# Modulation rows by column groups, half products ahead of the layer, and a new order on VectorE in a two-layer hybrid block

## The chip, the cores and the metric

One core of one Trainium2 chip. The metric is device time in microseconds; 2223.8 us is the median of three runs of the kernel before (2223.27 to 2225.72). A change of about 0.2% can be told from none.

## The reference, cut to what matters

```python
for i in range(DEPTH):                                   # 2 layers
    mod_l = (jax.nn.silu(c) @ w_mod[i] + b_mod[i])       # 6 x 1024 numbers, from one row
    mod_c = (jax.nn.silu(c_ctx) @ w_mod[i] + b_mod[i])   # the same for the context
    sh1, sc1, g1, sh2, sc2, g2 = jnp.split(mod_l, N_MOD, axis=-1)
    zl = _split_cols(_modulate(x, sh1, sc1) @ w_in[i])   # layernorm * (1 + sc1) + sh1
    zc = _split_cols(_modulate(h_ctx, csh1, csc1) @ w_in[i])
    # four mixers (retention, HGRN2, gated DeltaNet, RG-LRU) over context, then latents
    y_l = _merge([ret_l, hg_l, gd_l, lr_l], zl['merge_gate'], w_branch[i], w_out[i])
    x = _layernorm(alpha * x + g1 * y_l, ln_mix_g[i], ln_mix_b[i])
    f_l = _conv_ffn(_modulate(x, sh2, sc2), w_up[i], ffn_conv[i], ffn_conv_b[i], w_down[i])
    x = _layernorm(alpha * x + g2 * f_l, ln_ffn_g[i], ln_ffn_b[i])
    # the same for h_ctx in all layers but the last
```

There are 256 latent and 256 context tokens, D is 1024, the FFN 2816 wide. The gated DeltaNet's `qkv` columns go through a depthwise convolution over the tokens of a segment.

## The kernel before, in words

**Products.** Each large product streams one tile of weights (128 x 1024 numbers, 512 KB, tile `wraw`) from memory over SP's queue. ScalarE (ACT) copies it rounded into `wH` and VectorE (DVE) or GpSimd (POOL) subtracts to get the rest, `wL` (`splitter`, line 386). The activations `xm` are held as `xmH` and `xmL` (`xms` in layer 1). A product is then three passes: wH by xH, wH by xL, wL by xH. `gemm_ft` (line 687) puts weights in the array and streams tokens, `gemm_tf` and `gemm_tw` the other way round; results lie in three PSUM banks (`pgt`, line 520) until an **eviction** (`evac`, line 471) has read them: a convolution for `gft` and `up`, a residual add (`gy`, then `r`, then statistics `st`; `add_y`, line 945) for the `gtf` of w_out and w_down.

**The order is planned.** `pump` (line 297) writes one program order for each engine. Every piece of work is a generator (thread) that yields the engine and tiles it next needs; `account` keeps a clock for each engine, `when` (line 337) says when a thread could go on, and `pump` takes the one with the smallest start, less a lead and less the thread's fourth entry, its priority, if it is ready by the time the engine is free. Before, only the layernorm threads (`LN_FIRST`, 1.0) have a priority. Jobs of products run in the order of a list; a job at the head of it that is not `ready` holds back all behind it. `_Job.strict` stops a later one from overtaking.

**Modulation.** `mod_jobs` (line 781): silu(c) is a column pair `cz`, padded to 32; w_mod comes in 24 blocks (`nb` 0 to 11 of each layer) of 512 columns, each in four jobs. A job streams 256 columns for four parts of the contraction at once, each part into its own 32 partitions of the PSUM tile `modp`. After the fourth job ACT copies `modp` (128 x 512) to `modrow`, and the four parts are summed by products with a selection matrix `sel`: four products into `modcp` where the result is needed as columns (shift and scale, then DVE's `modc`), one into `modr` where it is needed as a row (the gates, then `modbm` to memory). Blocks 0, 2, 1, 3 of layer 0 are the head (`early`); 13 blocks are fillers, one job after each weight tile; blocks 6 and 7 of layer 1 come behind the first `up` jobs of layer 0, 4 and 5 at the start of layer 1, 9 to 11 in its middle (`LATE`).

**Head and layernorms.** `modulate` (line 851) does statistics, normalises, transposes (`xmt`) and modulates two segments, sg 0 the context and sg 1 the latents, eight blocks of 128 channels each. In layer 0 the first products are six of the gated DeltaNet, each as a pair (`both`, line 1793): first the context's 256 tokens, then the latents' with the weight tile loaded and split a second time. At the end of a sublayer `mid` and `end` (lines 1235 and 1249) do post-layernorm and `modulate` of segment 0 while the last product of segment 1 is on TensorE (PE).

All instructions go through one wrapper, so the profile puts them on line 85: rows are told apart by tile names.

Of the kernel before, what the change touches and what calls it, by code (L numbers as in the profile page):

```python
# [35 lines left out]
NWR = 4  # L36
# [12 lines left out]
LN_FIRST = 1.0  # L49
SPLIT_FIRST = 0.0  # L50
# [10 lines left out]
NBR = (1, 2)  # L61
NIN = (6, 5)
# [55 lines left out]
class Net:  # L118
    def __init__(self, nc, tc, I, out, n_tiles, dbg=None, stop=None):
        self.nc, self.tc, self.I, self.out = nc, tc, I, out  # L120
        self.specs = []
        self.n_tiles = n_tiles
        self.dbg = dbg or {}
        self.stop = stop
        self.PE, self.A, self.V = _Eng(self, nc.tensor, "PE"), _Eng(self, nc.scalar, "ACT"), _Eng(self, nc.vector, "DVE")
        self.G, self.S = _Eng(self, nc.gpsimd, "POOL"), _Eng(self, nc.sync, "SP")
        self.clk = dict(PE=0.0, ACT=0.0, DVE=0.0, POOL=0.0, SP=0.0, DMA=0.0)
        self.rdy, self.rd, self.base, self.slots, self.hw, self.by_seg, self.sto = {}, {}, {}, {}, 0.0, set(), {}
        self.table, self.n_ran = "exp", 0
# [4 lines left out]
        self.raws, self.plain, self.open, self.ok, self.masks_ok = 0, False, {}, set(), False  # L134
        self.want, self.dma_q, self.ready_q, self.n_wt = [], [], [], 0

# [200 lines left out]
    def when(self, t):  # L337

        w = t[1]
        if callable(w):  # L340
            return "PE", (0.0 if w() else None)
        key, w = w[:2] if isinstance(w, tuple) else ("PE", w)
        if key == "tt":
            key = "DVE" if self.clk["DVE"] < self.clk["POOL"] + 1.0 else "POOL"
        return key, max([max(self.after(self.rdy, y, key), self.base.get(y, 0.0)) for x in (w or []) for y in self.names(x)] + [0.0])
# [22 lines left out]
    def feed(self):  # L368

        while len(self.want) + len(self.dma_q) + len(self.ready_q) < (10 if self.jobs and self.jobs[0].early else 4):  # L370
            if not self.pick():
                break
        while self.want and self.raws < (8 if self.want[0][1].early else NWR):
# [9 lines left out]
            self.dma_q.append((raw, w, job.mode))  # L383
            self.raws += 1

    def splitter(self):

        while True:
            yield lambda: len(self.ready_q) < NWH - 1 and len(self.dma_q) > 0
            raw, w, mode = self.dma_q.pop(0)  # L390
            if mode == "plain":
                self.ready_q.append((raw, None))
# [8 lines left out]
            self.ready_q.append((H, L))  # L401
# [27 lines left out]
    def next_tile(self):  # L429
        if self.plain:  # L430
# [5 lines left out]
        self.plain = r[1] is None  # L436
        self.feed()
        return r
# [32 lines left out]
    def evac(self, rec, ps, f, eng="ACT"):  # L471

        job = self.cur
        job.pend += 1

        def run():
            yield eng, [ps]
            r = f(ps)
            if r is not None:
                yield from r  # L480
            job.pend -= 1
        t = self.spawn(run())
        rec.append(t)
        t[2] = True
# [74 lines left out]
    def load_consts(self):  # L559
# [4 lines left out]
        self.sel_c = const.tile([128, 2], F32, name="sel")  # L564
        S.dma_start(self.sel_c, I["c_sel"])
# [121 lines left out]
    def gemm_ft(self, ps, HL, xH, xL, K, w=128, c0=0):  # L687
# [4 lines left out]
        for k in range(K):  # L692
            h = H[:, k * w + c0:k * w + c0 + 128]
            for p, x in enumerate(xH(k) + xL(k)):

                mm(ps[:, x[1]:x[1] + x[0].shape[-1]], h, x[0], start=(k == 0 and p == 0), stop=False)
            n += 2
            if n % 4 == 0:
                yield
        for k in range(K):  # L700
            xs = xH(k)
            for p, x in enumerate(xs):
                mm(ps[:, x[1]:x[1] + x[0].shape[-1]], L[:, k * w + c0:k * w + c0 + 128], x[0], start=False,
                   stop=(k == K - 1 and p == len(xs) - 1))
# [4 lines left out]
    def in_ft(self, i, c0, tsl, evac, cond=None):  # L709
# [9 lines left out]
        jb.ready = self.seen(i, 0, tsl.start, tsl.stop)  # L719
        return jb  # L720
# [60 lines left out]
    def mod_jobs(self, i, nb, early=False):  # L781
# [4 lines left out]
        def mk(kk):  # L786
            def run():
                if kk == 0:
                    if early:
                        st["row"] = self.tile(self.fw, [128, 512], F32, "f_row", "modrow", 4)  # L790
                        st["ps"], st["rec"] = self.pgt([128, 512], "modp")
                    else:
                        if self.mod_th is not None:
                            self.finish(self.mod_th)
                        st["row"] = None
                        st["ps"], st["rec"] = self.tile(self.pq, [128, 512], F32, "modp", "modp", 1), []
                W, ps = self.next_tile()[0], st["ps"]
                half, kh = kk % 2, kk // 2
# [9 lines left out]
            def evac(ps):  # L808
                row = st["row"] if early else self.ev([128, 512], "modrow")
                self.A.activation(row, ps, AF.Copy)  # L810
                kind = nb // 2
                if kind in (2, 5):
                    half, c0 = kind // 3, (nb % 2) * 512
                    yield "PE", [row], "free"
                    pr = self.pmt([128, 512], "modr")
                    mm(pr[0:2, :], self.sel_c, row, start=True, stop=True)
# [4 lines left out]
                    self.V.tensor_tensor(bm, bm, pr[0:2, :], op=ALU.add)  # L821
# [3 lines left out]
                yield "PE", [row], "free"  # L825
                kind = {0: 0, 1: 1, 3: 2, 4: 3}[kind]
                pc = self.pmt([128, 4, 2], "modcp")
# [4 lines left out]
                self.V.scalar_tensor_tensor(self.modc[i][:, kind, j0:j0 + 4, :], in0=pc, scalar=float(kind % 2),  # L832
                                            in1=self.par[i][:, b0:b0 + 4].unsqueeze(2).broadcast_to([128, 4, 2]), op0=ALU.add, op1=ALU.add)
            j = _Job([(("w_mod", i, nb * 512 + (kk % 2) * 256, 4, 256, (kk // 2) * 4), 1024)], run)
# [16 lines left out]
    def modulate(self, i, half, sg, xs):  # L851
# [25 lines left out]
        for d in range(0, 8, 2):  # L877
# [19 lines left out]
            self.tt(L, x32, H.bitcast(F32), op=ALU.subtract)  # L897
            yield xn
# [46 lines left out]
    def add_y(self, cs, sg, js, ps, al, stats):  # L945
# [9 lines left out]
        V.tensor_tensor(tmp, ps, self.grow[sg][:, cs].unsqueeze(1).broadcast_to([128, n, 512 // n]), op=ALU.mult)  # L955
        V.scalar_tensor_tensor(r, in0=r, scalar=al, in1=tmp, op0=ALU.mult, op1=ALU.add)
# [16 lines left out]
    def body(self):  # L973
# [11 lines left out]
        xs = {}  # L985
        for sg, nm in ((0, "ctx"), (1, "x")):
# [3 lines left out]
        self.A.dma_start(self.ck, self.I["c_f32"])  # L990
# [4 lines left out]
        self.fill = rest  # L995
# [790 lines left out]
    def gdn_jobs(self, inst, g):  # L1786
# [6 lines left out]
        def both(make, t0):  # L1793

            if g == 0 and t0 == 0:
# [6 lines left out]
        for m, dst in ((g, ("yqk", 0)), (2 + g, ("yqk", 1)), (4 + 2 * g, ("yv", 0)), (5 + 2 * g, ("yv", 1))):  # L1802
            def make(t0, t1, m=m, dst=dst):
# [10 lines left out]
                return self.in_ft(i, COL["gdn_qkv"] + m * 128, slice(t0, t1), ev, cond)  # L1814
# [363 lines left out]
N_TILES = 485 + 2 * SPLIT_UP  # L2178
# [9 lines left out]
def _constants():  # L2188
# [22 lines left out]
    sel = np.zeros((128, 2), np.float32)  # L2211
    for j in range(2):
        sel[j::32, j] = 1.0
    c["c_sel"] = sel
# [33 lines left out]
def _host_arrays(a, specs):  # L2248
# [13 lines left out]
    for i in range(DEPTH):  # L2262
# [19 lines left out]
        for d in range(2):  # L2282
            for ty, nm in enumerate(("lru_w_a", "lru_w_i")):
# [11 lines left out]
               c_msk=(128, 416), c_sel=(128, 2), c_rope=(128, 2, 256),  # L2295
# [25 lines left out]
```

## Time and profile before

| | |
|---|---|
| median of three runs | 2223.8 us |
| the profiled execution, its own time | 2219.78 us |
| its span, first to last instruction | 2218.0 us |
| mean granted TensorE clock | 0.965 of 2.4 GHz |
| busy: PE, DVE, ACT, POOL | 2039.0, 1495.4, 868.6, 427.3 us |

The rows further down are from this one execution. A row of a timeline gives start, length, engine, operation, result <- operands, shape, count, and in brackets the idle time just before with what ended it. Matmul lengths overlap: the cost of one in a stream is the distance of two starts.

### The profile page before, as it was taken

To read this page: it belongs to the slowest core of one execution; us is meant where nothing else is said; L and a number is where in the kernel's file an instruction comes from. 1 tells how busy PE (TensorE), PEld (TensorE's weight loads), DVE (VectorE), ACT (ScalarE), POOL (GpSimd) and SP (SyncE) were. 2 spreads that over 40 slices of the span, in tenths; PEclk is the share of its full clock that TensorE was granted. 3 is DMA by queue.
4 is the path that set the end of the run, shared out by engine and by line. 5 is a ranking of instruction groups with operands and counts; after the bars stand their busy time and mean duration, and the time that the engine had idled before them with its cause. 6 is when DMAs were issued, how large, how long until landed. Compare 5 with 4: busy or idle time off the path is not lost. (4 is left out here: it accounts for less than half of the span.)

```text
span 2218.0 us, 33680 instructions
## 1 busy us (share of the span) xinstructions
PE 2039.0 (92%) x13236; PEld 1749.5 (79%) x13236; DVE 1495.4 (67%) x2520; ACT 868.6 (39%) x1277; POOL 427.3 (19%) x442
## 2 busy tenths in 40 slices
PE   6999999999999999789999976998989999879997
PEld 4766777788889878678898865887978989867895
DVE  6787565445738368986646678787476566778786
ACT  4555331322222323344314434556332333326562
POOL 0163216220101001200000022273225221200000
PEclk9999999999999999889999998999999999989999
DMA  7544434424141567462223244354324422566553
GB/s 298 201 133 150 154 124 129 129 98 140 67 136 64 170 217 241 148 218 95 98 93 98 97 147 166 108 169 119 120 96 130 142 72 63 184 245 229 176 185 109
DMA packets 129679, 319.35 MB, mean 144 GB/s; under 512 B 29136, under 2 KB 51568, under 8 KB 129520
## 3 DMA queue, kind: packets, MB, share of 16 engines
q1 hardware_dynamic: 128000, 312.17, 42.7%
q0 software_dynamic: 832, 2.54, 0.4%
q8 instruction: 104, 1.70, 0.3%
q10 hardware_dynamic: 688, 2.49, 0.3%
q14 instruction: 55, 0.45, 0.1%
HBM read 294.05 MB, written 23.10 MB: 143 GB/s over the span
## 5 line engine op out<-in xcount | busy, mean ns | idle before, releaser
L85 DVE TENSOR_TENSOR wL<-wraw,wH 128x1024 fp32r<-128x1024 f32 (+2 forms) x339 | 419.4, 1242 | 172.9 <-ACT wH L85 167.6
L85 ACT ACTIVATE wH<-wraw 128x1024 fp32r<-128x1024 f32 (+1 forms) x395 | 407.9, 1036 | 233.3 <-PE gtf L85 150.7
L85 POOL TENSOR_TENSOR wL<-wraw,wH 128x1024 fp32r<-128x1024 f32 (+2 forms) x56 | 131.5, 2350 | 933.7 <-ACT wH L85 860.0
L85 PE MATMUL gft<-xmH,wH 128*128 128x512 f32 (+1 forms) x544 | 215.4, 400 | 7.4 <-DVE g_th L85 3.8
L85 PE MATMUL gft<-xmL,wH 128*128 128x512 f32 (+1 forms) x544 | 205.2, 382 | 0.0
L85 PE MATMUL gft<-xms,wH 128*128 128x256 f32 x1344 | 188.5, 292 | 8.0 <-DVE gd_yv L85 2.8
L85 PEld LDWEIGHTS gft<-xms,wH 128*128 128x128 f32 x1344 | 173.5, 197 | 15.4 <-issue 11.2
L85 DVE SCALAR_TENSOR_TENSOR ffy<-up,parf,ffy 128x255 f32<-128x255 f32 (+1 forms) x188 | 110.8, 589 | 74.7 <-ACT ffy L85 70.3
L85 PE MATMUL up<-xmL,wH 128*128 128x512 f32 (+1 forms) x400 | 144.4, 369 | 3.5 <-DVE xmL L85 3.5
L85 PE MATMUL up<-xmH,wH 128*128 128x512 f32 (+1 forms) x400 | 144.0, 368 | 0.0
L85 PEld LDWEIGHTS gft<-xmH,wH 128*128 128x128 f32 x544 | 103.1, 190 | 46.7 <-issue 17.5
L85 PE MATMUL gft<-xmH,wL 128*128 128x512 f32 (+1 forms) x544 | 133.2, 383 | 1.2 <-DVE wL L85 0.9
L85 PE MATMUL gtf<-wH,hidH 128*128 128x256 f32 (+1 forms) x352 | 114.4, 341 | 16.4 <-DVE gy L85 15.7
L85 PE MATMUL gtf<-wH,xmH 128*128 128x256 f32 (+1 forms) x384 | 109.8, 313 | 13.9 <-DVE gy L85 11.9
L85 PEld LDWEIGHTS gft<-xmL,wH 128*128 128x128 f32 x544 | 103.3, 190 | 17.4 <-issue 0.7
L85 PEld LDWEIGHTS gft<-xmH,wL 128*128 128x128 f32 x544 | 97.3, 189 | 20.9 <-DVE wL L85 1.1
L85 PE MATMUL gtf<-wH,hidL 128*128 128x256 f32 (+1 forms) x352 | 113.8, 340 | 0.0
L85 PE MATMUL gtf<-wH,xmL 128*128 128x256 f32 (+1 forms) x384 | 106.1, 303 | 0.0
L85 PE MATMUL gft<-xms,wL 128*128 128x256 f32 x672 | 99.1, 293 | 5.0 <-POOL wL L85 4.9
L85 ACT ACTIVATE ffy<-up,parf 128x256 f32<-128x256 f32 (+1 forms) x94 | 61.3, 652 | 107.4 <-PE up L85 106.8
L85 PE MATMUL up<-xms,wH 128*128 128x256 f32 x704 | 93.0, 285 | 2.0 <-ACT wH L85 1.8
L85 PE MATMUL mg_b<-brH,wH 128*128 128x256 f32 (+1 forms) x288 | 89.8, 332 | 5.2 <-ACT brH L85 3.1
(327 smaller groups left out, 4291.7 us busy)
## 6 DMA issues: line engine op xcount, KB each, us to landing
wraw<-in_wt SPq DMA_DIRECT2D x475, 512.0 KB
thd<-mg_t SPq DMA_DIRECT2D x32, 256.0 KB
mg_th<-thd SPq DMA_DIRECT2D x32, 256.0 KB
lnw<-in_rows SPq DMA_DIRECT2D x8, 512.0 KB
thd<-mg_t SPq DMA_DIRECT2D x32, 128.0 KB
xmm<-thd SPq DMA_DIRECT2D x16, 256.0 KB
brd<-ro_b SPq DMA_DIRECT2D x28, 128.0 KB
ret_tab<-in_c_ret SPq DMA_DIRECT2D x16, 192.0 KB
```

The lines of the kernel that those rows point to most:

```text
L85: r = f(*a, **k)
```

## The change

- A modulation job now holds two parts of the contraction and all 512 columns; each 128 columns go to their own 32 partitions of a 128 x 128 `modp`. Eight matmuls of 128 columns take the place of four of 256. Nothing is left to sum: `modrow` is 128 x 128, `modcp` is one PE transposition, `modr` four matmuls of 128 columns with two columns of the identity each. `sel` and its load are gone. The head's blocks share the one `modp` tile with the others, and a block's first job first finishes the block before.
- Three of the gated DeltaNet's tiles in layer 0 (`HEAD`) are computed in two halves: `head_ft` over the first four channel blocks as soon as these are modulated for both segments, `rest_ft` over the others. Two halves stand before block 3 of the modulation, one after it. In layer 0 the pairs are gone: all 512 tokens are one job, and seven weight tiles are not loaded a second time (481 tiles with the three more of the halves, 485 before).
- Evictions get priority 2.0 (`EVAC_FIRST`). `add_y` yields between its product and its sum, `modulate` between the statistics of its blocks.
- The transposition of a block that is not early may follow 3 us later (`LATER`).
- The constants `ck` are loaded on ACT's queue ahead of the two inputs instead of behind them. Early tiles have a count of buffers of their own (`raws0`).

```diff
+EVAC_FIRST = 2.0
+LATER = 3.0
+HEAD = tuple(COL["gdn_qkv"] + m * 128 for m in (0, 2, 4))
...
+        lag = w[3] if isinstance(w, tuple) and len(w) > 3 else 0.0
...
-        return key, max([...] + [0.0])
+        return key, max([...] + [0.0]) + lag
...
-        while len(self.want) + len(self.dma_q) + len(self.ready_q) < (10 if self.jobs and self.jobs[0].early else 4):
+        while len(self.want) + len(self.dma_q) + len(self.ready_q) < (10 if self.head else 4):
...
-        t = self.spawn(run())
+        t = self.spawn(run(), EVAC_FIRST)
...
-    def gemm_ft(self, ps, HL, xH, xL, K, w=128, c0=0):
+    def gemm_ft(self, ps, HL, xH, xL, K, w=128, c0=0, first=True, last=True):
...
+    def head_ft(self, c0):
+        def run():
+            HL = self.next_tile()
+            self.parts[c0] = self.pgt([128, 512], "gft")
+            yield from self.gemm_ft(self.parts[c0][0], HL, *self.xf(0, 512), 4, last=False)
+        jb = _Job([(("w_in", 0, c0, 4, 128, 0), 512)], run)
+        jb.ready = lambda: all((0, 0, sg, "half") in self.ok for sg in range(2))
+        return jb
+    def rest_ft(self, c0, evac, cond):
+        def run():
+            HL = self.next_tile()
+            ps, rec = self.parts.pop(c0)
+            xs = [lambda k, x=x: x(k + 4) for x in self.xf(0, 512)]
+            yield from self.gemm_ft(ps, HL, *xs, 4, first=False)
+            self.evac(rec, ps, evac)
...
-                for k in range(4):
-                    mm(ps[32 * k:32 * k + 32, half * 256:half * 256 + 256], self.cz[:, kh * 4 + k, :], W[:, k * 256:(k + 1) * 256],
-                       start=(kk == 0), stop=(kk == 3))
+                for k in range(2):
+                    for j in range(4):
+                        mm(ps[32 * j:32 * j + 32, :], self.cz[:, kk * 2 + k, :], W[:, k * 512 + j * 128:k * 512 + (j + 1) * 128],
+                           start=(kk == 0 and k == 0), stop=(kk == 3 and k == 1))
...
-                    mm(pr[0:2, :], self.sel_c, row, start=True, stop=True)
+                    for j in range(4):
+                        mm(pr[0:2, j, :], self.ident[:, 32 * j:32 * j + 2], row, start=True, stop=True)
...
-                yield "PE", [row], "free"
+                yield "PE", [row], "free", 0.0 if early else LATER
...
-                for j in range(4):
-                    mm(pc[:, j, :], row[:, j * 128:(j + 1) * 128], self.sel_c, start=True, stop=True)
+                self.PE.transpose(pc.rearrange("p j c -> p (j c)"), row, self.ident)
...
                 V.bn_stats(st[:, j, q, :], xs[j][:, q * 512:(q + 1) * 512])
+            yield "DVE", [st]
...
+            if d == 2:
+                self.ok.add((i, half, sg, "half"))
...
         V.tensor_tensor(tmp, ps, self.grow[sg][:, cs].unsqueeze(1).broadcast_to([128, n, 512 // n]), op=ALU.mult)
+        yield "DVE", [tmp], "free"
...
+        hd = [self.head_ft(c0) for c0 in HEAD]
+        early[12:12] = hd[:2]
+        early.append(hd[2])
...
-            if g == 0 and t0 == 0:
+            if g == 0 and t0 == 0 and i > 0:
...
+                return self.rest_ft(c, ev, cond) if i == 0 and c in HEAD else self.in_ft(i, c, slice(t0, t1), ev, cond)
```

## Rows read from the trace of the kernel before

**Rows 1.** The page's part 1: engine, busy us, share, instructions.

```profile
PE 2039.0 (92%) x13236; PEld 1749.5 (79%) x13236; DVE 1495.4 (67%) x2520; ACT 868.6 (39%) x1277; POOL 427.3 (19%) x442
```

**Rows 2.** The waits of PE: total us, times, longest.

```profile
PE gtf L85 <- DVE gy L85: 27.7, 6, 11.9
...
PE modr L85 <- ACT modrow L85: 12.8, 2, 12.0
...
PE modcp L85 <- ACT modrow L85: 7.3, 7, 1.8
...
PE gft L85 <- DVE g_th L85: 6.3, 3, 2.5
```

**Rows 3.** PE's timeline in the head, 21 to 48 us.

```profile
21.74 1.08 PE L85 MATMUL modp<-wraw,cz 128*32 128x256 f32 x8 [0.20 <-DMA wraw<-in_wt]
22.75 1.87 PE L85 MATMUL modcp<-sel,modrow 128*128 128x2 f32 x8
...
35.35 1.94 PE L85 MATMUL modp<-wraw,cz 128*32 128x256 f32 x32
38.00 1.05 PE L85 MATMUL modcp<-sel,modrow 128*128 128x2 f32 x8 [0.72 <-ACT modrow L85]
38.92 1.94 PE L85 MATMUL xmt<-ck,x 128*128 128x128 f32 x16
...
44.34 0.39 PE L85 MATMUL gft<-xmH,wH 128*128 128x256 f32 x1 [2.91 <-ACT wH L85]
...
47.97 0.64 PE L85 MATMUL modp<-wraw,cz 128*32 128x256 f32 x8
```

**Rows 4.** DVE's timeline in the head: last of the first and of the second half.

```profile
35.42 0.69 DVE L85 TENSOR_TENSOR xmL<-xm,xmH 128x512 fp32r<-128x512 f32 x1
...
47.24 0.99 DVE L85 TENSOR_SCALAR xm<-xmt,modc 128x256 f32<-128x256 f32 x2
```

**Rows 5.** PE's groups by form: matmuls into 64 partitions at a time; busy, mean ns.

```profile
L85 PE MATMUL gd_pw<-gd_T,gd_ek 128*64 128x128 f32 x128 | 8.8, 279 | 0.1
```

**Rows 6.** The timeline around the layernorm behind w_out of layer 0.

```profile
902.89 2.43 POOL L85 TENSOR_TENSOR wL<-wraw,wH 128x1024 fp32r<-128x1024 f32 x1 [0.26 <-ACT wH L85]
...
903.10 2.24 DVE L85 TENSOR_TENSOR rq<-rq_i 128x2 f32<-128x2 f32 x1
...
920.85 0.80 PE L85 MATMUL gtf<-wH,xmH 128*128 128x512 f32 x1 [11.94 <-DVE gy L85]
...
933.35 0.69 DVE L85 TENSOR_TENSOR xmL<-xm,xmH 128x512 fp32r<-128x512 f32 x1
...
935.15 0.28 PE L85 MATMUL up<-xmH,wH 128*128 128x256 f32 x1
...
939.42 0.99 DVE L85 SCALAR_TENSOR_TENSOR ffy<-up,parf,ffy 128x255 f32<-128x255 f32 x2
```

**Rows 7.** The timeline from the last products of layer 0 into layer 1.

```profile
1298.26 1.23 DVE L85 TENSOR_TENSOR wL<-wraw,wH 128x1024 fp32r<-128x1024 f32 x1 [0.41 <-ACT wH L85]
...
1300.23 0.47 PE L85 MATMUL gtf<-wH,hidH 128*128 128x512 f32 x1 [1.47 <-DVE gy L85]
...
1325.74 0.77 PE L85 MATMUL gtf<-wH,hidH 128*128 128x512 f32 x1 [9.87 <-DVE gy L85]
...
1338.22 0.69 DVE L85 TENSOR_TENSOR xms<-xm,xms 128x512 fp32r<-128x512 f32 x1
...
1343.47 2.08 PE L85 MATMUL gft<-xms,wH 128*128 128x256 f32 x16
...
1370.85 1.01 PE L85 MATMUL modr<-modrow,sel 128*2 128x512 f32 x1 [12.03 <-ACT modrow L85]
...
1381.45 1.22 PE L85 MATMUL gft<-xms,wH 128*128 128x256 f32 x4 [2.21 <-ACT wH L85]
```

**Rows 8.** Busy us by stretch: length, PE, PEld, DVE, ACT, POOL; granted clock, DMA, GB/s.

```profile
1301.00:1384.40 83.40, 56.10 (x326) 42.00 (x325) 72.43 (x134) 29.93 (x47) 25.71 (x12) 0.86 0.44 144
901.00:975.00 74.00, 54.46 (x343) 45.19 (x342) 68.40 (x123) 28.82 (x43) 15.94 (x7) 0.81 0.48 164
```

More of the change, by code (lines that the diff above doesn't have):

```diff
@@ L344, in when @@
             key = "DVE" if self.clk["DVE"] < self.clk["POOL"] + 1.0 else "POOL"
-        return key, max([max(self.after(self.rdy, y, key), self.base.get(y, 0.0)) for x in (w or []) for y in self.names(x)] + [0.0])
+        return key, max([max(self.after(self.rdy, y, key), self.base.get(y, 0.0)) for x in (w or []) for y in self.names(x)] + [0.0]) + lag
     def take(self, j):
@@ L382, in feed @@
             self.n_wt += 1
-            self.dma_q.append((raw, w, job.mode))
-            self.raws += 1
+            self.dma_q.append((raw, w, job.mode, job.early))
+            if job.early:
+                self.raws0 += 1
+            else:
+                self.raws += 1
     def splitter(self):
@@ L435, in next_tile @@
         r = self.ready_q.pop(0)
-        self.plain = r[1] is None
+        self.plain = r[1] is None and ("early" if r[2] else "late")
         self.feed()
-        return r
+        return r[:2]
     def drain(self, jobs):
@@ L694, in gemm_ft @@
             for p, x in enumerate(xH(k) + xL(k)):
-                mm(ps[:, x[1]:x[1] + x[0].shape[-1]], h, x[0], start=(k == 0 and p == 0), stop=False)
+                mm(ps[:, x[1]:x[1] + x[0].shape[-1]], h, x[0], start=(first and k == 0 and p == 0), stop=False)
             n += 2
@@ L703, in gemm_ft @@
                 mm(ps[:, x[1]:x[1] + x[0].shape[-1]], L[:, k * w + c0:k * w + c0 + 128], x[0], start=False,
-                   stop=(k == K - 1 and p == len(xs) - 1))
+                   stop=(last and k == K - 1 and p == len(xs) - 1))
             n += 1
@@ L719, in in_ft @@
         jb.ready = self.seen(i, 0, tsl.start, tsl.stop)
+        return jb
[6 more added lines that the diff above has]
+        jb.ready = lambda: all((0, 0, sg, "half") in self.ok for sg in range(2))
+        return jb
+    def rest_ft(self, c0, evac, cond):
[5 more added lines that the diff above has]
+            self.evac(rec, ps, evac)
+        jb = _Job([(("w_in", 0, c0, 4, 128, 4), 512)], run, cond)
+        jb.strict = True
+        jb.ready = self.seen(0, 0, 0, 512)
         return jb
@@ L788, in run @@
                 if kk == 0:
[L789 to L796, printed above, removed]
+                    if self.mod_th is not None:
+                        self.finish(self.mod_th)
+                    st["ps"], st["rec"] = self.tile(self.pq, [128, 128], F32, "modp", "modp", 1), []
                 W, ps = self.next_tile()[0], st["ps"]
-                half, kh = kk % 2, kk // 2
-                for k in range(4):
-                    mm(ps[32 * k:32 * k + 32, half * 256:half * 256 + 256], self.cz[:, kh * 4 + k, :], W[:, k * 256:(k + 1) * 256],
-                       start=(kk == 0), stop=(kk == 3))
+                for k in range(2):
+                    for j in range(4):
+                        mm(ps[32 * j:32 * j + 32, :], self.cz[:, kk * 2 + k, :], W[:, k * 512 + j * 128:k * 512 + (j + 1) * 128],
+                           start=(kk == 0 and k == 0), stop=(kk == 3 and k == 1))
                 if kk == 3:
@@ L808, in evac @@
             def evac(ps):
-                row = st["row"] if early else self.ev([128, 512], "modrow")
+                row = self.tile(self.fw, [128, 128], F32, "f_row", "modrow", 4) if early else self.ev([128, 128], "modrow")
                 self.A.activation(row, ps, AF.Copy)
@@ L813, in evac @@
                     half, c0 = kind // 3, (nb % 2) * 512
-                    yield "PE", [row], "free"
-                    pr = self.pmt([128, 512], "modr")
-                    mm(pr[0:2, :], self.sel_c, row, start=True, stop=True)
+                    yield "PE", [row], "free", LATER
+                    pr = self.pmt([128, 4, 128], "modr")
+                    for j in range(4):
+                        mm(pr[0:2, j, :], self.ident[:, 32 * j:32 * j + 2], row, start=True, stop=True)
                     bm = self.ev([2, 512], "modbm")
@@ L819, in evac @@
                     yield "DVE", [bm, pr]
-                    self.V.tensor_tensor(bm, bm, pr[0:2, :], op=ALU.add)
+                    self.V.tensor_tensor(bm, bm, pr[0:2].rearrange("p j c -> p (j c)"), op=ALU.add)
                     self.V.tensor_scalar(bm, bm, 0.5, None, op0=ALU.mult)
@@ L994, in body @@
         self.close(self.fw)
-        self.fill = rest
+        self.fill, self.head = rest, False
         self.S.dma_start(self.msk.bitcast(F32), self.I["c_msk"])
```

36 lines of the change are left out of this document (16 added, 20 removed).

## The prediction

> **What bounds the kernel now.** First the page's busy shares: PE is busy 92% of the span [rows 1], so some 180 us of it can be won without making products cheaper. Then the waits of PE, to see behind whom they lie: the residual add `gy` (27.7 us, of which one wait is 11.9), the modulation row `modrow` (12.8 and 7.3 us), `g_th` (6.3 us) [rows 2]. These are the waits at which the change aims. Then the timeline around the long ones, and there the reader is to see what comes next. The 11.94 us behind `gy` end at 920.85, but the first `up`, for which w_out is only in the way, starts at 935.15, and its last operand `xmL` is written at 933.35 plus 0.69 [rows 6]. The layernorm's chain on DVE ends with PE's work, stall included. The same in layer 0's end: a wait of 9.87 us ends at 1325.74, the last `xms` of segment 0 comes at 1338.22, the first product of layer 1 at 1343.47; then 12.03 us behind `modrow`, and the latents' products only at 1381.45 [rows 7]. Last the busy times of the two stretches: DVE is busy 68.4 of 74.0 us and 72.4 of 83.4 [rows 8]. **In both DVE's work, not its order, is nearly the bound**; 5.6 and 11.0 us are idle.
>
> **The sum** is made against the profiled execution's 2219.78 us (span 2218.0 and 1.8 around it); the median is 4.0 above it. What the sum changes I take off the median.
>
> *Modulation, sums gone.* A `modcp` of four products takes PE from 38.00 to 38.92, so 0.92 us; a transposition costs a sixteenth of 1.94, 0.12 [rows 3]. 0.8 us are saved each of 16 times. Four are in the head (below), three (blocks 6, 7, 9 of layer 1) where PE waits anyway: 9 x 0.8 = **-7.2**. `modr` streams 512 columns before and after: 0, at most eight more short records, under 1 us. `modrow` and its PSUM read shrink to a quarter; ACT is 39% busy, so 0 outside the head.
>
> *Modulation, more matmuls.* A job has 16 records instead of 8, each half as long. Four jobs of 8 records take 1.94 us, one alone 0.64, so a job in a stream costs (1.94 - 0.64) / 3 = 0.43 [rows 3]. The columns streamed are the same, so no gain. For a loss, the nearest row with 128 columns goes two groups at a time: 8.8 us / 128 = 69 ns each [rows 5]; by the 0.43 us it would be 53, so 16 ns are extra, times 16 records 0.25 us a job, times 52 filler jobs 13 us. I take 0.05 us a job, since the row with four groups shows nothing extra: **+2.6**, with 0 and +13 as ends. The other 44 jobs lie in the head, where a tile lands every 1.28 us (1.08 busy and 0.20 of waiting) and a job takes 1.08 [rows 3], or where PE waits for DVE.
>
> The Trainium skill (TensorE: Matmul & The Clock Gate, LDWEIGHTS) says that a load of weights takes its columns divided by 1.2 in ns, 27 ns for 32, which speaks against the change: it makes twice as many. If none were hidden, my estimate from that page is 8 x 27 ns x 52 = 11.2 us in the place of 2.6, and the sum would be -12.3. The trace's 0.43 us a job says that they are hidden when four groups run in turn.
>
> *The head.* Before, PE does its first real product at 44.34 [rows 3], though the first half of the channels is modulated for both segments at 35.42 + 0.69 = 36.1; the second half ends about 48.9 (47.24, 0.99 and the 0.69 of an `xmL`) [rows 4]. In the chain to the first half, `modcp` costs 1.87 us [rows 3], twice: some 2.5 us fall away, and ACT reads a quarter. So halves start at about 34. One is 12 matmuls of 512 columns; 16 of 256 take 2.08 [rows 7], 1.92 without the tail, so 12 of twice the width some 2.8 us. But two of them now stand on PE ahead of block 3, whose jobs ran at 35.35: its `modcp` ends at about 42 instead of 39 (38.00 and 1.05), and the second half at about 50 instead of 48.9. The context's pairs, which ran from 44.34, have to wait for that too. At 50 PE has done 8.4 us of halves where before it had done 5.8 (two context products), and from there all weights lie ready and both segments with them, where before PE stalled several times. The pairs gone spare some 1.5 us of PE, seven splits and half the fixed cost of three convolution steps on DVE. I take **-4** (ends -9 and +4: block 3 later still). Moved queues: `ck` ahead of `ctx` and `x` on ACT's queue puts 384 KB before them, 0.75 of the 1.28 us in which a tile lands [rows 3]: statistics begin 1 us later, hidden by the modulation's tiles, the eighth of which is used at 21.74 [rows 3]; without that cover 1 us. On SP's queue two half tiles stand ahead of block 3's last tiles, also some 1.3 us, and are in the 42 above.
>
> *Transpositions later.* The 7.3 us that `modcp` waits for `modrow` are seven waits of at most 1.8 [rows 2]; some lie in the head and next to layernorms. Where PE is the bound: **-1.8**, ends 0 and -3. The 12.03 us stay outside: the next block needs the one `modp` tile, so the row must be read first, and PE has no real product before 1381.45.
>
> *Evictions first, behind w_out.* `gy` would go at about 909 instead of 920, so the 11.94 us [rows 6] go. Late next is the layernorm: its chain now has three more evictions ahead of it (each three steps of 512 columns, 0.69 us a step as the `xmL` of that width, 2.1 in all) and, since PE does not stop, POOL's splits beside it. A `rq` of two numbers took 2.24 us beside such a split [rows 6]. So PE waits for `xmL` instead, and `up` starts at 935 to 943; but segment 1's evictions are done earlier, which gives time back by 975. **-1**, ends -5 (DVE's idle time) and +8.
>
> *The same at the end of layer 0 and into layer 1.* 9.87 us go, PE then waits for the `xms` of 1338.22 [rows 7]; segment 1's layernorm starts some 10 us earlier, in a stretch where DVE has 11.0 us idle of 83.4 [rows 8]. **-5**, ends -11 and +3. The statistics in steps only let an eviction between blocks: 0 by themselves.
>
> *Other evictions.* Four times `gy` waits for a split started just before it (1.23 us at 1298.26, PE stalls 1.47) [rows 7]. Priority counts only when the eviction is ready as DVE falls free, and there it was not: **-1.5** of 5.9, ends 0 and -5.9. `g_th` waits behind mixer steps: **-3** of its 6.3 us [rows 2], ends 0 and -6.3. The mixers, whose readouts and masks go behind evictions now: 0, with +-8, since the whole order is planned anew.
>
> Sum: -7.2 + 2.6 - 4 - 1.8 - 1 - 5 - 1.5 - 3 = **-20.9**; 2223.8 - 20.9 = **2203**. Its own range, from ends that don't all fall together, is 2190 to 2216.
>
> **The rivals.**
> *The stalls are won whole.* 11.94 + 9.87 + 12.03 = 33.8 us go instead of 6: -48.7, 2175. For it: the waits are there. Against: DVE's 68.4 of 74 [rows 8]. 10%.
> *The priority seldom acts,* since evictions are seldom waiting when DVE falls free: what is left is -7.2 + 2.6 - 4 - 1.8 = -10.4, 2213. 15%.
> *The loads of weights show.* +13 instead of +2.6: -10.5, 2213. 10%. (By the Trainium skill's rule above it would be 2212.)
> *Splits starve (slower).* In layer 1 a tile of `up` is 24 matmuls of 256 columns, 2.9 us at 0.12. DVE gives each 1.23 for `wL` [rows 7] and 0.99 for two convolution steps [rows 6], and has 0.7 left for the gate's products and for ports held by POOL. If evictions always go ahead, the split is always last and PE waits for `wL`. From 0.58 us a tile on, 44 tiles give back all and 4.4 more; at 0.7 it is +31, and the time 2234. Against: three tiles are split ahead. 15%.
>
> **How the numbers follow.** Forecast 50%, rivals 10, 15, 10 and 15. A measurement of this kernel can tell about 0.2%, 4.4 us, from no change. Faster by more: nearly all of the forecast, the first rival, four fifths of the next two, none of the last: 0.78. Within: 0.10. Slower by more: 0.12. The range leaves out most of the first and the last rival: 2183 to 2223.
>
> **What would show it.** Right: PE's waits for `gy` and `g_th` shrink and waits for `xmL`, `xms` or `xn` grow in their place; `gft` starts near 34 to 37 us, with an idle stretch before 50; 16 records of `modp` in 0.45 to 0.5 us in a stream. Wrong: `up` at 920 us in the old count (the first rival); `modp` at 0.6 us or more (the third); PE waits for `wL` of 20 us and more in layer 1 (the last).

## The result, and the profile after

The changed kernel takes **2201.3 us** (median of four runs, 2195.2 to 2206.1); the kernel before, beside it on the same chip, 2223.5 us. The ratio is 0.9894 with an interval of 0.9875 to 0.9913: about 1.1% faster, and within 2 us of the 2203 predicted. The profiled execution is the lowest of the four, 2195.15 us, so what follows shows some 6 us more of a gain than the median does. The runs of the changed kernel lie 11 us apart, those of the one before 4.

The page's busy time of the engines, to be held against [rows 1]:

```profile
span 2193.4 us, 34754 instructions
PE 2023.3 (92%) x13820; PEld 1752.4 (80%) x13820; DVE 1478.5 (67%) x2491; ACT 849.5 (39%) x1259; POOL 436.4 (20%) x440
```

PE is busy 15.7 us less than before (2039.0), and the span is 24.6 us shorter. The waits of PE, as total, times and longest, which answer to [rows 2]:

```profile
PE gd_Tt L91 <- DVE gd_T L91: 14.8, 3, 8.8
PE modcp L91 <- ACT modrow L91: 12.0, 5, 9.6
PE gtf L91 <- DVE gy L91: 9.2, 2, 7.5
PE up L91 <- DVE xmL L91: 6.9, 6, 2.0
PE modr L91 <- ACT modrow L91: 4.9, 2, 4.5
```

and one more line of the kernel before, whose three waits all lie in layer 1's mixers:

```profile
PE gd_Tt L85 <- DVE gd_T L85: 9.6, 3, 7.0
```

The waits for `gy` fell from 27.7 to 9.2 us, those before `modr` from 12.8 to 4.9, and `g_th` is gone from the list. Two long waits are new: 9.6 us before a `modcp` in the head, and 8.8 us before `gd_Tt` in layer 0's mixers, where the kernel before has no such wait. Cut at the first or last start of a tile's products on PE (from the span's start to the first `gft`, then last `gft` of layer 0, last `mg_b`, first and last `up`, and again in layer 1), the two profiled executions and those of the experiments split into stages like this. Each number is the length of a stage, the difference of two starts in the trace, each rounded to 0.1 us:

```
us                head  mixers0 merge0 w_out0   up0  between  mixers1 merge1 w_out1
before            44.3   731.7   96.0   63.1   328.1   80.3    517.8   93.6   53.5
changed           35.6   739.1   97.4   58.4   333.0   73.0    506.7   94.1   46.2
e1_head_whole     31.8   740.7   98.6   58.7   333.3   73.0    510.1   95.0   46.9
e2_evac0          35.3   731.7   97.3   59.7   331.8   79.2    524.9   94.5   55.4
e3_later0         35.8   745.5   99.4   59.3   334.8   74.2    513.4   97.1   45.6
e4_steps_off      30.5   741.3   98.3   57.1   333.2   78.8    512.5   94.7   44.6
e5_no_halves      45.1   742.6   99.2   59.2   334.3   72.9    515.5   95.7   46.6
e6_order_noise    35.6   746.4   97.0   58.4   332.3   73.3    510.6   94.6   45.3
e7_before_evac    44.7   752.1   94.4   61.3   339.9   78.3    516.5   95.3   48.0
e8_add_whole      36.0   741.4   98.2   62.4   328.6   74.2    518.7   96.4   48.2
e9                35.2   732.0   97.3   58.5   333.0   73.0    512.6   96.4   50.7
e10               30.5   740.2   97.7   58.8   335.8   73.3    510.4   94.5   47.9
e11_cols_only     39.7   744.0   98.2   61.6   327.7   80.1    525.9   92.3   52.6
e12               45.1   731.8   95.4   61.3   331.6   79.4    515.8   95.2   46.7
```

Each row is one execution: the lowest of its kernel's runs for the changed kernel, e7, e10 and e12, the highest for e3 to e6 and e8. How much of a row is the execution's own can be read where several kernels have the same order of instructions on all four engines. In layer 0's mixers that is so for the kernel before and e12 (731.7 and 731.8 us), for e2 and e9 (731.7 and 732.0), and for the changed kernel, e1, e4 and e8 (739.1 to 741.4). So the length of that stage goes with the order, to within some 2 us. In layer 1's mixers e1 has the changed kernel's order but for one place on PE and one on DVE, and takes 510.1 us against 506.7.

The first two lines say where the time came from. **At 1263 us, more than half of the way, the changed kernel has won nothing**: 8.7 us in the head and 4.7 at w_out were given back in the mixers (7.4), the merge (1.4) and the up-projection (4.9). The gain at w_out only moves the first `up`: from the last merge product to the last `up` it is 391.2 us before and 391.4 after. The 24.6 us are won behind it: 7.3 between the layers, 11.1 in the mixers of layer 1 (some 3 of them of this execution, as e1's 510.1 says), 7.3 from its last merge product to its first `up`; the stages that are left out give about 1 us back.

What held the head and layer 0's mixers up can be read from two places. First PE in the head, with the idle time in brackets, and DVE and ACT at that time:

```profile
14.70 1.08 PE L91 MATMUL modp<-wraw,cz 128*32 128x128 f32 x16 [1.50 <-DMA wraw<-in_wt]
25.36 0.47 PE L91 MATMUL modcp<-ck,modrow 128*128 128x128 f32 x1 [9.58 <-ACT modrow L91]
...
13.55 1.28 DVE L91 BATCH_NORM_STATS2 bst<-x 128x6 f32<-128x512 f32 x2
18.05 3.66 DVE L91 BATCH_NORM_STATS2 bst<-x 128x6 f32<-128x512 f32 x6 [3.22 <-DMA x<-in_x]
23.71 0.16 DVE L91 SCALAR_TENSOR_TENSOR ln_nb<-mv,rq_n 128x2 f32<-128x2 f32 x1
...
23.91 1.24 ACT L91 ACTIVATE x<-x,ln_nb,rq_n 128x1024 f32<-128x1024 f32 x1 [11.66 <-DMA wraw<-in_wt]
25.05 0.26 ACT L91 ACTIVATE modrow<-modp 128x128 f32<-128x128 f32 x1
```

The context's statistics pause behind their first pair; what comes next on DVE waits 3.22 us for the latents' rows to land. So `ln_nb` starts only at 23.71 us, ACT's normalisation stands until it is there (the view puts that wait down to a transfer, but it ends 0.04 us behind `ln_nb`), and `modrow` stands behind it on ACT's queue. PE has no other `modp` tile to write and stops for 9.58 us.

The second place is in layer 0's mixers, on DVE and on PE, and then the busy time by stretch (length, PE, PEld, DVE, ACT, POOL; granted clock, DMA share, GB/s):

```profile
177.93 0.91 DVE L91 COPY gd_T<-gd_Z 32x128 f32<-32x128 f32 x4 [8.61 <-DMA gd_Z<-blk]
178.90 2.35 PE L91 MATMUL gd_Tt<-ck,gd_T 128*128 128x128 f32 x8 [8.84 <-DVE gd_T L91]
...
160.00:169.70 9.70, 9.70 (x69) 7.36 (x68) 9.07 (x10) 3.18 (x4) 8.84 (x12) 1.00 0.42 135
169.70:178.90 9.20, 0.36 (x3) 0.01 (x1) 0.87 (x4) 0.09 (x1) 3.62 (x11) 0.64 0.47 81
178.90:183.00 4.10, 3.98 (x16) 3.25 (x17) 1.23 (x1) 3.17 (x7) 0.00 (x0) 0.56 0.93 341
183.00:187.00 4.00, 4.00 (x34) 3.72 (x33) 0.52 (x1) 0.60 (x1) 0.00 (x0) 1.00 0.55 156
```

The gated delta net's inverse is made on POOL, written out and read back by a transfer, and copied to `gd_T` by DVE and ACT. The written order has the transposition `gd_Tt` next on PE when the transfer is still under way: PE, DVE and ACT stand, and the products behind it run at a granted clock of 0.56 of 2.4 GHz on the mean of 4.1 us.

### The profile page after: what moved, and what is told of

It reads as the page before. It is cut to its first block, busy times and chain, and to the rows that moved or that the text cites. A ratio compares the mean times of both kernels' runs of the same rounds, so it can differ in the third digit from the quotient of the medians.

```text
span 2193.4 us, 34754 instructions
## 1 busy us (share of the span) xinstructions
PE 2023.3 (92%) x13820; PEld 1752.4 (80%) x13820; DVE 1478.5 (67%) x2491; ACT 849.5 (39%) x1259; POOL 436.4 (20%) x440
## 5 line engine op out<-in xcount | busy, mean ns | idle before, releaser
L91 DVE TENSOR_TENSOR wL<-wraw,wH 128x1024 fp32r<-128x1024 f32 (+1 forms) x326 | 405.5, 1250 | 154.7 <-ACT wH L91 154.5
L91 ACT ACTIVATE wH<-wraw 128x1024 fp32r<-128x1024 f32 (+2 forms) x391 | 401.7, 1032 | 233.9 <-PE gtf L91 146.0
L91 POOL TENSOR_TENSOR wL<-wraw,wH 128x1024 fp32r<-128x1024 f32 (+1 forms) x65 | 148.2, 2284 | 1131.6 <-ACT wH L91 1078.5
L91 PE MATMUL gft<-xmH,wH 128*128 128x512 f32 x512 | 211.0, 412 | 0.8 <-ACT wH L91 0.8
L91 PE MATMUL gft<-xmL,wH 128*128 128x512 f32 x512 | 203.4, 397 | 3.7 <-DVE xmL L91 3.7
L91 PE MATMUL gft<-xmH,wL 128*128 128x512 f32 x512 | 132.8, 398 | 0.0
L91 PEld LDWEIGHTS gft<-xmH,wH 128*128 128x128 f32 x512 | 97.5, 190 | 28.9 <-issue 8.6
L91 ACT ACTIVATE ffy<-up,parf 128x256 f32<-128x256 f32 (+1 forms) x94 | 61.3, 652 | 145.7 <-PE up L91 145.6
L91 PEld LDWEIGHTS gft<-xmL,wH 128*128 128x128 f32 x512 | 97.7, 191 | 23.6 <-DVE xmL L91 5.3
L91 PEld LDWEIGHTS up<-xmL,wH 128*128 128x128 f32 x400 | 78.6, 197 | 20.1 <-DVE xmL L91 8.3
```

Of the source, the lines that this page charges most:

```text
L91: r = f(*a, **k)
```

## The experiments

Twelve kernels ran, three groups of four on three chips. The ratio to the kernel before on the same chip is the measure, since its median went from 2223.5 to 2227.0 us between chips; the changed kernel's is 0.9894.

**e1_head_whole**: the first layernorm's statistics in one go.

```diff
-            yield "DVE", [st]
+            if (i, half) != (0, 0):
+                yield "DVE", [st]
```

> Only the first layernorm (layer 0, both segments) takes its statistics in one go again; the later ones keep the steps. Theory A: the steps let x's two bn_stats pairs go between ctx's statistics and ctx's short chain behind them, so that ln_nb came at 23.71 instead of 14.31 us, modrow waited behind the normalisation on ACT, and PE stood 9.58 us at 25.36 us. Then that wait is gone (under 2 us), the second modc and the first half products start 6 to 9 us sooner than in the changed kernel. How much of it is left at the end is open in A: the lead of layer 0 vanished by 1261 us in the changed kernel, so A says 2196 to 2201 us (median). Rival: the wait hangs on ACT's or the transfers' order and not on the statistics; then a wait of 7 us or more stays in the first 40 us and the time stays within 2198 to 2205 us.

Measured: 2199.3 us, 0.9889 [0.9869, 0.9910]. The 9.58 us are gone (`modcp` waits 5.2 us in three times in the first 60), `ln_nb` comes at 17.85 us, and the first product 3.8 us sooner, not the 6 to 9 of theory A. So the steps did make that wait. But at the last `up` of layer 0 the run stands at 1263.1 us, the changed kernel at 1263.5. The lead is lost, and the total is the same. In layer 0's mixers all four engines have the changed kernel's order, so it is not a new order that takes the lead back: 1.6 us go in the mixers and 1.2 in the merge.

**e2_evac0**: no head start for evictions.

```diff
-EVAC_FIRST = 2.0
+EVAC_FIRST = 0.0
```

> The eviction's head start in the planner is 0 instead of 2.0. Theory A: the priority brought what was won from 1261 us on (9.87 us on gy at the end of layer 0 became 5.3 us in two waits, the waits on gy through layer 1 went from 27.7 to 9.2 us in sum): without it waits on gy are back above 20 us in sum and the time is 2208 to 2215 us. Rival: the waits left because the additions wait in a step of their own and the transpositions come later; then waits on gy stay under 13 us and the time within 2196 to 2206 us.

Measured: 2224.0 us, 0.9995 [0.9983, 1.0007]: without this one number the whole gain is gone, 22.7 us by the medians, more than theory A said. The waits for `gy` came back to 17.5 us, not to above 20:

```profile
PE gtf L91 <- DVE gy L91: 17.5, 6, 7.8
PE modr L91 <- ACT modrow L91: 8.7, 2, 8.3
PE gft L91 <- DVE g_th L91: 4.4, 3, 2.0
```

By stages it is 6.2 us between the layers, 18.2 in layer 1's mixers, 9.2 at its w_out, and 7.4 the other way in layer 0's mixers. In layer 1's mixers the listed waits of PE are 11.4 us longer (55.1 against 43.7) and PE is busy 6.7 us more (469.69 against 463.04) at a granted clock of 0.94 against 0.96. The sum of the waits does not set that clock: the kernel before has 55.9 us of them in that stage, at 0.96 (PE busy 461.51).

**e3_later0** and **e6_order_noise**: the fillers' lag.

```diff
-LATER = 3.0
+LATER = 0.0
```

> The lag of the fillers' transpositions is 0 instead of 3.0 us. Theory A: the 12.03 us wait for modrow between the layers became 4.49 us because the transposition was put later; with lag 0 it is 9 to 12 us again, the sum of the modcp and modr waits is 8 to 12 us above the changed kernel's, and the time is 2204 to 2210 us. Rival: the eviction's priority shortened it (modrow is an eviction on ACT); then that wait stays under 6 us and the time within 2196 to 2206 us.

Measured: 2209.1 us, 0.9940 [0.9920, 0.9960], so 8 to 10 us are lost, but not as theory A had it: the wait between the layers did not come back (3.5 us at most), and the waits for `modrow` are only 3.3 us longer in sum. The loss in the stages is layer 0's mixers, 6.4 us, and layer 1's, 6.7.

```diff
-LATER = 3.0
+LATER = 2.5
```

> The lag is 2.5 instead of 3.0 us, an edit with no meaning of its own: it moves the planner's order here and there. Theory A: the planner's order alone is worth up to 5 us either way, so 2196 to 2206 us, with milestones in layer 0 shifting by some us. Rival: the plan is stable and the time is the changed kernel's to within 1 us.

Measured: 2200.6 us, 0.9892 [0.9867, 0.9918]: no change in the time, though layer 0's mixers were as long in its profile (746.4) as with lag 0. Its instructions stand in another order there than the changed kernel's. So the planner's order moves a stage by 7 us for an edit without a meaning, where executions of one order lay 2 us apart, and of e3's loss only the 3.3 us of waits can be put to the lag.

**e7_before_evac**: the kernel before with the head start alone.

```diff
+EVAC_FIRST = 2.0
...
-        t = self.spawn(run())
+        t = self.spawn(run(), EVAC_FIRST)
```

> The kernel before with the eviction's head start of 2.0 alone; columns, halves, steps and lag as before. The changed kernel with the head start at 0 took 2224.0 us, as long as the kernel before, so the head start is worth 22 to 23 us there. Theory A: it is worth that by itself, since evictions free the PSUM banks and make gy's transpositions early everywhere: 2200 to 2208 us. Rival: it pays only beside the steps and the lag, because without them DVE's long uncut stretches (bn_stats pairs, scale and addition of add_y) keep an eviction waiting whatever its rank: 2214 to 2224 us, with waits on gy above 20 us in sum.

Measured: 2244.1 us, 1.0076 [1.0057, 1.0096], slower than either theory allowed. What is worth 22.7 us in one kernel costs 17 in the other. It is layer 0's mixers, 20.4 us longer; the waits in that stage include 10.5 us for `gd_T`; the kernel before has none there.

**e8_add_whole**: the gate's product and the addition in one step.

```diff
-        yield "DVE", [tmp], "free"
```

> The product with the gate row and its addition to the residual are one step again. Theory A: the split lets an eviction of gy go between them, up to 1 us for each of the waits on gy, and those are 9.2 us in sum now: 2201 to 2207 us, waits on gy 12 to 20 us in sum. Rival: evictions go first without it, the split does nothing: 2196 to 2203 us with waits on gy under 11 us.

Measured: 2211.9 us, 0.9933 [0.9913, 0.9952]. Theory A's direction and waits (13.7 us on `gy`), at more than its price: 9 us by the ratios. At w_out of layer 0 it is 4.0 us (62.4; the four other kernels without the split have 61.3 to 63.1, all with it 57.1 to 59.7), but the up-projection behind it is 4.4 us shorter, so nothing of that is lost in the end. Of the 12 us in layer 1's mixers 8 come at once: the latents' normalisation `xn` starts 36.2 us into the stage (1377.02) and in the changed kernel 28.4 us into it (1364.83). These are its waits for what the layernorms write:

```profile
PE xmt L91 <- DVE xn L91: 9.8, 3, 3.5
PE gft L91 <- DVE xms L91: 7.0, 5, 2.0
```

The changed kernel has 1.2 us of the first and none of the second. So the addition in one piece holds the latents' layernorm up as well; the other 4 us stay open.

**e4_steps_off**: no layernorm in steps (the line of e1 taken out).

> No layernorm takes its statistics in steps. The same undone in the first layernorm alone took 2199.3 us (changed kernel 2201.3). Theory A: behind layer 0's w_out and between the layers the four bn_stats pairs of 1.4 us keep evictions of gy waiting, so the wait of 7.5 us at 916 us becomes 9 to 12 us and those between the layers grow by 3 to 6 us: 2203 to 2210 us. Rival: the statistics cost nothing there, since xn's normalisation behind them is the later one: 2194 to 2202 us.

Measured: 2200.1 us, 0.9872 [0.9850, 0.9893]: the time is the rival's, though theory A was right about one of the two waits on `gy`: between the layers it is 11.1 us (1.7 in the changed kernel; theory A had it grow by 3 to 6), while the one at 916 us stays at 7.3, where theory A had 9 to 12. Between the layers the run takes 78.8 us, not 73.0; the head takes 30.5, not 35.6. The two nearly cancel.

**e5_no_halves**: no half products in the head, and the pairs again.

```diff
-HEAD = tuple(COL["gdn_qkv"] + m * 128 for m in (0, 2, 4))
+HEAD = tuple(COL["gdn_qkv"] + m * 128 for m in ())
...
-            if g == 0 and t0 == 0 and i > 0:
+            if g == 0 and t0 == 0:
```

> The in-projection's first three column blocks run whole again, with the pairs of the kernel before; all else as in the changed kernel. Theory A: layer 0 gives its lead back before 1263 us whatever the head does, so the first products come 7 to 9 us later than in the changed kernel, and the time is 2197 to 2206 us, as the changed kernel's. Rival: the head's lead is carried to the end: 2206 to 2212 us.

Measured: 2218.3 us, 0.9962 [0.9949, 0.9974]: 15 us by the ratios. Theory A falls, and the rival's 2212 us is passed too; this lead is carried to the end, where e1's was not. Of the 26.9 us between the profiled spans (2220.3, the highest of its runs, and 2193.4, the lowest) the head has 9.5 and the mixers 3.5 and 8.8. Halves and pairs were taken out together, so the price is that of both.

**e9_evac_not_in_mix0** and **e10_mix0_head**: evictions first everywhere but in layer 0's mixers; e10 has e1's edit too.

```diff
...
-        t = self.spawn(run(), EVAC_FIRST)
+        t = self.spawn(run(), self.evf)
...
+        self.evf = EVAC_FIRST if i else 0.0
         self.brd = [self.dr.tile([128, 4, 512], F32, name=f"brd{i}_{j}") for j in range(4)]
...
         self.pump(lambda: all(t[0] is None for t in ts) and all(j.done for j in inst_jobs))
+        self.evf = EVAC_FIRST
```

> The changed kernel with the head start of evictions at 0 from the opening of layer 0's mixers to their end, at 2.0 elsewhere. In the run with 0 everywhere the mixers of layer 0 (first product to last gft) took 731.7 us, in all runs with 2.0 739 to 752 us, with a wait of 8 to 12 us for gd_T that is under 1 us without the head start. Theory A: the eviction's priority costs 5 to 8 us in layer 0's mixers and wins behind them; so the wait for gd_T goes, the last gft of layer 0 comes at 767 to 770 us, and the time is 2192 to 2198 us. Rival: the planner's order shifts and gives it back in layer 1, as the head's lead was given back: 2198 to 2206 us.

> The same, and the first layernorm takes its statistics in one go. Theory A: each won some us in its own stretch (5 us in the head, 7 in the mixers), and with the evictions last in the mixers nothing there takes the head's lead away: 2188 to 2194 us. Rival: the head's lead is lost in layer 0 whatever the order: as the run beside it, within 3 us.

Measured: e9 2198.1 us, 0.9882 [0.9866, 0.9899]; e10 2201.1 us, 0.9900 [0.9882, 0.9919]. In e9 the mixers took 732.0 us as expected, and the transposition that had waited 8.84 us runs without a wait at full clock:

```profile
191.74 1.03 PE L91 MATMUL gd_Tt<-ck,gd_T 128*128 128x128 f32 x8
```

But of the 7.5 us by which it enters layer 1 sooner (1329.0 against 1336.5) 3 are left in the median, no more than the intervals hide, so both theories' bounds are touched and neither is shown. e10 misses theory A by 7 us. There, with the same rank of evictions, the wait for `gd_T` is back (5.3 us, longest 4.9) and the stage takes 740.2. So the head start is not the wait's only cause: with the head's edit the planner writes another order in that stage than e9's. What all 14 profiles agree on is the wait itself, though that is an agreement and not a test of its cause: where `gd_Tt` waits 1.1 us or less in that stage (before, e2, e9, e12) it takes 731.7 to 732.0 us, in the ten others 739.1 to 752.1 (in e3 with 2.8 us there and another wait, 8.8 us before `lru_gp`, for which the trace names no releaser).

**e12_before_evac_late**: e7 with e9's lines.

> The kernel before with the head start of 2.0 alone, and that at 0 in layer 0's mixers. With 2.0 everywhere it took 2244.1 us, 17 us more than the kernel before. Theory A: all of that was layer 0's mixers (20 us longer there); behind them the head start wins by itself what it won in the changed kernel at the three transitions (7 us between the layers, 7 at w_out of layer 1): 2206 to 2214 us. Rival: without statistics in steps, additions in two and later transpositions it wins nothing there: 2219 to 2230 us.

Measured: 2216.3 us, 0.9962 [0.9949, 0.9976], between theory A and its rival. Layer 0's mixers are back at 731.8 us; w_out of layer 1 is won (46.7), between the layers next to nothing (79.4). Its waits for `gy` and `modrow`:

```profile
PE gtf L86 <- DVE gy L86: 17.4, 2, 11.1
PE modr L86 <- ACT modrow L86: 6.1, 2, 5.4
```

The head start alone took four of the six waits for `gy`, and the 12.03 us before `modr` [rows 7] fell to 5.4. Of the two that are left, the one at w_out of layer 0 fell from 11.94 to 6.3 us; the one between the layers stayed (9.87 before, 11.1 now). Here is why, DVE and POOL ahead of it:

```profile
1309.59 9.62 POOL L86 TENSOR_TENSOR wL<-wraw,wH 128x1024 fp32r<-128x1024 f32 x3 [1.99 <-ACT wH L86]
...
1309.09 1.28 DVE L86 SCALAR_TENSOR_TENSOR r<-r,mv,lnw 128x1024 f32<-128x1024 f32 x1
1310.40 3.31 DVE L86 SCALAR_TENSOR_TENSOR r<-r,rq_n,lnw 128x1024 f32<-128x1024 f32 x1
1313.63 3.38 DVE L86 SCALAR_TENSOR_TENSOR r<-r,mv,lnw 128x1024 f32<-128x1024 f32 x1
1317.04 3.24 DVE L86 SCALAR_TENSOR_TENSOR r<-r,rq_n,lnw 128x1024 f32<-128x1024 f32 x1
1320.21 2.46 DVE L86 BATCH_NORM_STATS2 bst<-r 128x6 f32<-128x512 f32 x4
...
1324.81 0.68 DVE L86 TENSOR_TENSOR gy<-gtf,grow 128x512 f32<-128x512 f32 x1
```

and the same work in the changed kernel:

```profile
1311.43 1.28 DVE L91 SCALAR_TENSOR_TENSOR r<-r,rq_n,lnw 128x1024 f32<-128x1024 f32 x1
1312.63 1.28 DVE L91 BATCH_NORM_STATS2 bst<-r 128x6 f32<-128x512 f32 x2
1313.83 2.18 DVE L91 TENSOR_TENSOR wL<-wraw,wH 128x1024 fp32r<-128x1024 f32 x1
1315.92 1.27 DVE L91 BATCH_NORM_STATS2 bst<-r 128x6 f32<-128x512 f32 x2
1317.12 1.20 DVE L91 TENSOR_TENSOR wL<-wraw,wH 128x1024 fp32r<-128x1024 f32 x1
1318.25 1.28 DVE L91 TENSOR_TENSOR gy<-gtf,grow 128x512 f32<-128x512 f32 x2
```

In e12 the whole chain from the statistics to `ln_nb` runs ahead of `gy`; in the changed kernel splits and the eviction stand between its pieces. The three slow operations beside POOL are not the difference, for e8, with the steps, has them too (3.31, 3.38 and 3.24 us) and loses only 1.2 us in this stage (and 8 behind it, in the latents' layernorm). The stages say it: between the layers every kernel with both the head start and the steps takes 72.9 to 74.2 us, those with one of them or neither 78.3 to 80.3. Neither is worth more than 2 us there without the other.

**e11_cols_only**: the modulation's column groups alone (e5, with `EVAC_FIRST` and `LATER` 0 and the two added `yield` lines out; the constants' place on ACT's queue and the early tiles' buffers stay as in the changed kernel).

> The modulation's column groups alone: no halves, no steps, no split addition, lag 0 and head start 0. Theory A: one transposition in the place of four short products spares 0.3 to 0.6 us each of 16 times and modp costs nothing more, so 3 to 8 us at most: 2216 to 2222 us. Rival: its saving is given back like the rest of layer 0's: as the kernel before to within 3 us.

Measured: 2233.9 us, 1.0043 [1.0028, 1.0058]: 9.6 us slower, on the side that no theory had. PE's own work did shrink; the groups of `modp` and `modcp` (busy, mean ns, idle before), of this kernel and then of the kernel before:

```profile
L91 PE MATMUL modp<-wraw,cz 128*32 128x128 f32 x1536 | 66.8, 304 | 19.0 <-DMA wraw<-in_wt 18.8
L91 PE MATMUL modcp<-ck,modrow 128*128 128x128 f32 x16 | 5.1, 320 | 8.5 <-ACT modrow L91 8.5
```

```profile
L85 PE MATMUL modp<-wraw,cz 128*32 128x256 f32 x768 | 69.0, 442 | 20.6 <-DMA wraw<-in_wt 20.6
L85 PE MATMUL modcp<-sel,modrow 128*128 128x2 f32 x128 | 18.5, 267 | 7.3 <-ACT modrow L85 7.3
```

The 13.4 us of `modcp` are not seen in the time. Layer 0's mixers are 12.3 us longer: PE is busy 4.3 us less there (704.06 against 708.31), and its waits are 16.3 us longer (42.5 against 26.2), one of 12.9 us for `gd_T` among them. Layer 1's are 8.1 us longer, with PE busy 5.7 us more (467.19 against 461.51) at a granted clock of 0.94 against 0.96. It is not this one execution: e2, whose order on PE differs there in two places only, takes 524.9 us. Whether the columns or the order make it is not shown.

## Why the prediction was right, and where it was wrong

**The total was right, and its sum was not the reason.** It added the parts as if each kept its worth beside the others. By the ratios, taking out the head start, the lag, the split addition or the halves costs 22, 10, 9 and 15 us; these four make 56, and the whole change is worth 24. With columns alone the kernel is slower, with the head start alone too. Several terms were too small, one is not seen in the time, and the mixers moved by nearly as much as the whole sum; that it came out within 2 us is in good part luck.

*Modulation, sums gone* (-7.2): the size was right, 13.4 us over 16 times is 0.84 each against 0.8. The step that failed is that nine of the sixteen savings would be saved time: in layer 0's mixers PE did 4.3 us less and waited 16.3 longer (e11).

*Modulation, more matmuls* (+2.6): four jobs (64 records at 45.33 us) take 1.96 us and one takes 0.65, so a job in a stream costs 0.44, as before, and the sum of the group fell. Nothing is lost and the **third rival** falls. The Trainium skill (TensorE: Matmul & The Clock Gate, LDWEIGHTS) prices a load by its columns; of the 11.2 us estimated from that rule, were none hidden, the trace shows nothing.

*The head* (-4): first products at 35.64, within the 34 to 37 foretold. The 9.58 us behind the steps of the statistics were not in it ("0 by themselves" was said of layers' ends and not asked of the head). The first half took PE 6.8 us, not 2.8, with 1.9 us of waits for `xmL`, and block 3's `modcp` came at 48.24 us, not by 42; of the idle stretch foretold before 50 only those 1.9 us came. The worth of halves and pairs was mis-sized: about -15 (e5).

*Transpositions later* (-1.8): 3.3 us of waits; what e3 lost beyond that can't be told from the order's own moves.

*Behind w_out of layer 0* (-1): 0 by the last `up` (391.2 and 391.4 us). The stage itself is 4.7 us shorter, with the first `up` at 930.5, sooner than the 935 to 943 foretold and not at 920, so the **first rival** falls: PE's waits for `xmL` before `up` grew from 3.5 to 6.9 us as foretold, and 7.5 of the 11.94 us for `gy` are left. The split addition, which got no term, is most of the 4.7; the time given back by 975 us was foreseen, its size was not.

*End of layer 0* (-5): -7.3, by the head start and the steps together. Of the 9.87 us 1.71 are left, and PE waits 3.63 us for a `wL` just ahead of them (1316.06). "**DVE's work, not its order**" is the bound was wrong: from the same distance behind the last `up` to the same behind the latents' first product (1301.3 to 1375.7 us) DVE is busy 66.3 of 74.4 us, 6.1 less than before [rows 8], and idle 8.1, not 11.0. The order sets how long its operations take, for it sets which run beside a split on POOL: the 13 on `r` take 16.1 us there, before 21.0. Two of them in the kernel before:

```profile
1311.27 3.31 DVE L85 SCALAR_TENSOR_TENSOR r<-r,rq_n,lnw 128x1024 f32<-128x1024 f32 x1
1314.50 3.40 DVE L85 SCALAR_TENSOR_TENSOR r<-r,mv,lnw 128x1024 f32<-128x1024 f32 x1
```

In the changed kernel all eight of that shape take 1.28 us there. The 12.03 us before `modr` "stay outside" was wrong: `modrow` is an eviction, and the head start alone takes 6.6 us off it (e12).

*Evictions behind a split* (-1.5) and *`g_th`* (-3): both went whole, 12.2 us of waits for a term of 4.5. Of six waits for `gy` the four short ones are gone, in e12 too; "and there it was not" (said of an eviction's being ready as DVE falls free) failed. The last stretch of layer 1 before `up`, -7.3 by the head start (55.4 without it; 5.5 are left at the last `up`), had no term at all.

*Mixers* (0, with 8 either way): +7.4 and -11.1, together -3.7. The bound holds for the sum, not for layer 1 alone, and the two moves are as large as the rest of the sum. The **second rival** (the priority seldom acts) falls with e2. *Splits starve*, the slower rival, falls too: `up` never waits for `wL` in the changed kernel's list, and the waits for it elsewhere (`gft` 6.1 us, `gtf` 4.9) are as long as before (6.1 and 4.8).

## What to carry to other kernels

In a kernel whose order a planner writes, a part's worth is only known beside the others: take each out of the finished version, and change one number without a meaning to see how far the order alone moves a stage; kernels with the same order in a stage show what an execution adds by itself. A rank for urgent work can need short pieces ahead of it to pay, as between the layers here, and short pieces can cost elsewhere, as in the head. Time saved on the busiest engine is won only in stages where nothing else ends last; look for the one long wait that grows in its place.

## What the runs showed of the hardware

DVE's operation on two tensors of 128x1024 takes 1.28 us by itself (1311.43 in the changed kernel, POOL idle) and 3.24 to 3.38 us beside splits on POOL (e12). A split took 2.42 us at 1301.14, beside smaller operations of DVE, and 3.2 there (three in 9.62). It is nearly as if they took turns, for 1.28 and 2.42 make 3.70. The Trainium skill (SBUF — State Buffer, Who interferes with whom) says that a DVE instruction with two inputs in SBUF contends with a POOL instruction that reads SBUF; the trace agrees, and its price here is 2.0 us each time.

After PE stood still for 8.84 us the granted clock was 0.56 of 2.4 GHz in the next 4.1 us, near the lower level of 1.2 GHz, and then 1.00; eight transpositions took 2.35 us there and 1.03 in e9, where PE had been busy for the 5.7 us ahead of them at a clock of 1.00. So, as an estimate, that wait cost about 1.8 us more than itself (0.44 of 4.1 us).
